# Sixteen of a modulation's 48 dot products moved ahead of the first attention

## The chip, the core and the metric

The kernel runs on one core of a Trainium2 chip. The core has five engines with instruction streams of their own: TensorE (PE: matmuls), VectorE (DVE), ScalarE (ACT), GpSimd (POOL) and SyncE (SP), which here only issues transfers. Each stream is written down when the program is built; the engines meet at semaphores. The metric is device time in microseconds (us), lower is better.

## The reference, cut to what matters

The kernel computes a two-layer diffusion trunk over 1024 latent tokens and 256 context tokens of width 1024, all in float32. Each layer derives a shift, a scale and a gate from a conditioning vector, modulates its input with them, projects it to queries, keys, values and a gate path, runs a windowed attention, and closes with a projection and a LayerNorm.

```
silu_c = silu(c);  silu_cc = silu(c_ctx)
for i in range(2):
    shift, scale, gate       = split(silu_c  @ w_ada[i] + b_ada[i], 3)    # latent tokens
    shift_c, scale_c, gate_c = split(silu_cc @ w_ada[i] + b_ada[i], 3)    # context tokens
    u  = h  * (1 + scale)   + shift
    uc = hc * (1 + scale_c) + shift_c
    y, yc = mixer_a(u, uc, ...) if i == 0 else mixer_b(u, uc, ...)
    h  = layer_norm(alpha * h  + gate   * y,  ...)
    hc = layer_norm(alpha * hc + gate_c * yc, ...)    # first layer only
```

What the change moves is a part of `silu_c @ w_ada` and `silu_cc @ w_ada`: the first layer's gate and the second layer's shift and scale, 3 x 1024 numbers for each of the two vectors. None of them is needed before the first layer's attention is nearly over.

## The kernel before, in words

**Numbers as pairs.** Every matmul operand is split into a high and a low part, and a product is three matmuls (high x high, high x low, low x high). So most evacuations of a PSUM tile are a copy on ACT (the high part) and a subtraction on DVE (the low part).

**The start.** The first layer's shift and scale are made on PE while the input comes in by eight blocks of 128 rows (`hraw`, 128x1280, four buffers, tag "hraw"). `u_make` modulates each block and splits it; `k_mm` and `v_mm` accumulate the keys and the first four token blocks of the values. When the eighth block is through, the keys stand in four PSUM tiles (`kps`, names `kp0_0`, `kp0_1`, `kp1_0`, `kp1_1`, latent tokens) and in a part of `kc` (context tokens), and the first values in `vps`.

**Evacuation of the keys and the values.** `rope_evac` takes a key tile through a shuffle on DVE (L500, into `rb`), a product with the cosines on DVE (L501, into `ra`), a product with the sines on POOL (L502, `rb`), and a sum on DVE (L503). `k_store` splits the sum: ACT writes the high part (L511) and DVE the low part (L512) of a tile `st`, of which there are two, and SP issues its store to the buffer `kdA` in memory. `v_evac` does the same for values (ACT L270, DVE L271, store to `vdA`). Meanwhile PE runs `vproj_pieces`, the remaining values by three PSUM tiles `pv-1_2`, `pv-1_3`, `pv-1_4` of 48 matmuls each.

**The queries.** Then comes `qprojA(0)`, the first two heads' queries: PSUM tiles `pj8_0`, `pj8_1` (24 matmuls of 512 columns each) and `pj8_2` (24 of 256 columns), and behind it the gate path `pj10_0`, `pj10_1`, `pj10_2`. These tiles and the ones of keys and values come from one pool of four PSUM tiles of 512 columns (tag "one"), so each waits until a tile before it has been read out.

**The first attention** runs by eight pairs of heads p, twenty steps each: scores on PE (`S_A`), bias, mask and minimum on DVE (L322), exponential on ACT (L329), normalisation on POOL (L334), transposes on PE (`T_A`) and their split (ACT L345, DVE L347), then the values' product (`pvA`). It needs the keys back from memory (`k_load`, into `kA`) and the values (`v_loadA`). Between the steps PE is filled with the projections of this pair's gate and the next pair's queries. `merge` interleaves the two lists.

**The dot products.** The modulation's 3072 numbers per vector are rows of `wadaT` (24 blocks j of 128 rows). One `dot_half(h, j)` takes half h of the columns of block j: a load of 128x512 (256 KB) into `gw`, a multiplication with accumulation on DVE for the latent vector (L681), a multiplication in place on POOL for the context vector (L682), and its sum on ACT (L663). The 48 are laid between the attention's steps by `SEG`, the number for each pair of heads. At each half's first one the silu of both vectors is made in `gh`.

**What sets the order.** The program's text gives the order; the tile framework then places each engine's instructions by priorities and by its own estimates, except those in `keep_in_program_order`. It also chooses which buffer of a tag a tile gets. An engine never takes an instruction ahead of one that stands before it in its stream, and neither does SP.

Of the kernel before, what the change touches and what calls it, by code (L numbers as in the profile page):

```python
# [11 lines left out]
F32 = mybir.dt.float32  # L12
F32R = mybir.dt.float32r
BF16 = mybir.dt.bfloat16
AF = mybir.ActivationFunctionType
ALU = mybir.AluOpType
# [3 lines left out]
P = 128  # L20
D = 1024
S = 1024
C = 256
T = S + C
# [13 lines left out]

GATED_LAST = 1 << 20

SEG = (7, 7, 7, 7, 7, 7, 6, 0)


def f32(ap):
# [38 lines left out]
def build(tc, i, out):  # L83
    nc = tc.nc
    mm = nc.tensor.matmul
    dma = nc.sync.dma_start
# [25 lines left out]
    dcol = cp.tile([P, 32, 2], F32, name="dcol")  # L112
# [4 lines left out]
    vdA = dr.tile([T, 4, P], F32, name="vdA")  # L117
# [107 lines left out]
    def vproj_pieces(j0, u, evac, b0=0):  # L225

        pieces = []
        state = {}  # L230

        def piece(b, t, kq):
            def run():
                j1 = j0 + 4 if j0 >= 0 else 8
                if b == b0 and t == 0 and kq == 0:
                    w.split(j1)
                    w.load(j1 + 2)
                if b == 4 and t == 1 and kq >= 2:
                    w.split(j1 + kq - 1)
                if t == 0 and kq == 0:  # L240
                    state[b] = psone(f"pv{j0}_{b}")
                pt = state[b][:, t * 256 : (t + 1) * 256]
                tok = slice((2 * b + t) * P, (2 * b + t + 1) * P)
                for kt in (2 * kq, 2 * kq + 1):
                    hi, lo = w.got[j0 + kt // 2 if j0 >= 0 else VALUES[kt // 2]]
                    sl = slice((kt % 2) * 256, (kt % 2 + 1) * 256)
                    lh, ll = u.at(kt, tok)
                    mm(pt, lh, hi[:, sl], start=kt == 0 and t == 0, stop=False)
                    mm(pt, lh, lo[:, sl], start=False, stop=False)
                    mm(pt, ll, hi[:, sl], start=False, stop=kt == KT - 1 and t == 1)  # L250
                if t == 1 and kq == 3:
                    evac(state.pop(b), b)

            return (6 * 109, run)

        for bs in ((0, 1), (2,), (3,), (4,)) if b0 == 0 and j0 == pos["Bv", 0] else [(b,) for b in range(b0, 5)]:
            for kq in range(4):
                pieces += [piece(b, t, kq) for b in bs for t in range(2)]
        return pieces
# [4 lines left out]
    def v_evac(pl, vd):  # L264
        def evac(pt, b):
            st = st_tile(pl)
            for t in range(2):
                v = st[:, t].rearrange("p (h l d) -> p h l d", h=4, l=2)
                src = pt[:, t * 256 : (t + 1) * 256].rearrange("p (h d) -> p h d", h=4)
                nc.scalar.activation(v[:, :, 0, :], src, AF.Copy, scale=0.5)  # L270
                nc.vector.scalar_tensor_tensor(v[:, :, 1, :], src, 0.5, f32(v[:, :, 0, :]), ALU.mult, ALU.subtract)  # L271
            t0 = 2 * b * P
            dma(vd[t0 : t0 + 2 * P].rearrange("(t p) h e -> p t (h e)", p=P), f32(st))

        return evac
# [13 lines left out]
    def merge(att, fill, lead=0.0):  # L289

        ta = sum(a[0] for a in att) or 1.0
        tf = sum(f[0] for f in fill)
        ia = jf = 0
        ca = cf = 0.0
        while ia < len(att) or jf < len(fill):
            need = att[ia][2] if ia < len(att) and len(att[ia]) > 2 else 0
            if jf < len(fill) and (ia == len(att) or jf < need or cf - lead <= ca * (tf - lead) / ta):
                cf += fill[jf][0]
                fill[jf][1]()
                jf += 1  # L300
            else:
                ca += att[ia][0]
                att[ia][1]()
                ia += 1
# [161 lines left out]
    uA = Tokens(up, "uA")  # L466
    ap_, ap_st = pool("apool", "right")
    pp, pp_st = pool("p0", "right")
# [150 lines left out]
    for kt in range(-1, KT + 1):  # L619
        if kt + 1 < KT:  # L620
            for n in range(3) if kt < 0 else (kt + 3,) if kt + 3 < KT else ():
                mod_load(n, upto[n])
                if n == 0:
                    w.split(2)
            if kt == 0:

                u_make(0)
                k_mm(0, slice(0, 2))
            mod_rows(kt + 1)
            if kt == 0:  # L630
                k_mm(0, slice(2, 6), True)
        if kt > 1:
            k_mm(kt - 1)
        if kt + 1 < KT:
            mod(kt + 1)
        if kt == 0:
            k_mm(0, slice(6, None), True)
        if kt < 0:

            warm(vps[:, 0:512], 12)  # L640
        if kt > 0:
            v_mm(kt - 1)
        if kt < KT and kt >= 0:
            if kt:
                u_make(kt)
            w.split(upto[min(kt + 1, 7)])
    dma(ident, i["ident"])
    dma(lnc, i["lnc"])
    dma(cos, i["cos"])
# [7 lines left out]
    gh, sums = [], []  # L657
# [7 lines left out]
    def dot_half(h, j):  # L665
        def run():
            dot_sum()
            if j == 0:
                gh.clear()
                for v in range(2):  # L670
                    t = px.tile([P, 512], F32, tag=f"gh{v}", bufs=1, name="gh")
                    dma(t, bass.AP(i["cr"].tensor, v * D + h * 512, [[0, P], [1, 512]]))
                    th = px.tile([P, 512], F32, tag="gw", bufs=2, name="gth")
                    nc.scalar.activation(th, t, AF.Tanh, scale=0.5)
                    nc.vector.scalar_tensor_tensor(t, th, 1.0, t, ALU.add, ALU.mult)
                    gh.append(t)
            acc = dhalf if h else dcol
            t = px.tile([P, 512], F32, tag="gw", bufs=2, name="gw")
            dma(t, i["wadaT"][j, :, h * 512 : (h + 1) * 512])
            o = ap_.tile([P, 512], F32, tag="ra", bufs=1, name="gj")  # L680
            nc.vector.tensor_tensor_reduce(o, t, gh[0], 0.5, 0.0, ALU.mult, ALU.add, accum_out=acc[:, j, 0:1])  # L681
            nc.gpsimd.tensor_tensor(t, t, gh[1], ALU.mult)  # L682
            sums.append((t, acc[:, j, 1:2]))

        return (0.0, run, 0)
# [9 lines left out]
            nc.vector.scalar_tensor_tensor(colB[:, v, :], scale, 1.0, lnc[:, 1, :], ALU.add, ALU.mult)  # L695
            nc.vector.tensor_tensor(colB[:, v, :], colB[:, v, :], shift, ALU.add)

    dots = [dot_half(h, j) for h in range(2) for j in range(24)]
    evs = []
    for c, (t0, n) in enumerate(CHUNKS):  # L700
        for nt in range(2):
            pt = kps[c, nt] if c < 2 else kc[:, nt * C : nt * C + C]
            evs.append((1.0, lambda nt=nt, pt=pt, t0=t0, n=n: rope_evac(k_store(nt), pp, 2)(pt, t0, n)))
    merge(evs, [])
    for b in range(2):
        v_evac(pp, vdA)(vps[:, b * 512 : (b + 1) * 512], b)
    merge([], vproj_pieces(-1, uA, v_evac(pp, vdA), 2))
    pp_st.close()
    pq, pq_st = pool("attA", "right")

# [164 lines left out]
    for p in range(8):  # L875
# [6 lines left out]
        if p < 7:  # L882
            n = len(att)
# [77 lines left out]
    for b in range(10):  # L961
# [5 lines left out]
        else:  # L967
            o = og_split(up, raw, "h2") if b % 2 else og_split(oa, raw, "og")
# [8 lines left out]
        g = gts[:, b // 8]  # L977
# [287 lines left out]
    for n, row in enumerate(rowsB):  # L1265
        ex = []
        if n < len(subsB):
            h, jp, r = subsB[n]
# [209 lines left out]
```

## Time and profile before

| | |
|---|---|
| runs | 1424.73, 1422.10, 1424.25 us; median 1424.25 us |
| span of the profiled execution | 1422.0 us; the median of the runs is 2.25 us above it |
| PE, DVE, ACT, POOL busy over the span | 98%, 69%, 51%, 44% |
| keys' evacuation and values' projection | from 57 us to 78 us of the span |
| queries' projection up to the first scores | 78 us to 95 us |
| first attention | 95 us to some 580 us |
| the 48 dot products | first load at 106.0 us, last sum at 517.5 us |

Only the span of the profiled execution is given, not a time of its own for it; the three runs and the span lie within 2.7 us. A row of the profile's timeline has the start, the duration, the engine, the line of the program, the operation and its tiles (written <- read, buffer numbers left out). A duration begins when the engine takes the instruction up, so it holds whatever the instruction waits for after that.

### The profile page before, as it was taken

What the parts mean: (1) busy time and instruction counts of PE and PEld (TensorE: products, weight loads), DVE (VectorE), ACT (ScalarE), POOL (GpSimd) and SP (SyncE); (2) the same over time, 40 slices, a digit from 0 to 9 for tenths busy, and PEclk for the clock granted to TensorE, in tenths of its full rate; (3) what the DMA queues carried; (4) which work ended last, traced back from release to release, by engine and by line L of the source; (5) the groups of instructions that cost most, each with busy time, mean ns of one, the idle gap of its engine ahead of it and who ended that gap; (6) DMA issues with size and microseconds to landing.
All of it is one profiled execution on the core that took longest, in us unless ns stands there. A gap on an engine that the chain in (4) does not pass through costs nothing. (4 is left out here: it accounts for less than half of the span.)

```text
span 1422.0 us, 25163 instructions
## 1 busy us (share of the span) xinstructions
PE 1386.9 (98%) x8816; PEld 1215.3 (85%) x8816; DVE 981.9 (69%) x2220; ACT 731.0 (51%) x1560; POOL 627.5 (44%) x776
## 2 busy tenths in 40 slices
PE   9999999999999999999999999999999999999996
PEld 6988898888988888888898899888988899887885
DVE  4658887878888788666433765565565565669598
ACT  4347776677776778432222555455455454558200
POOL 0326676667667667233311333333233232325583
PEclk9999999999999999999999999999999999999998
DMA  9472114123222124344287575465555564475763
GB/s 380 180 222 86 61 50 131 47 79 101 72 71 64 57 69 144 123 134 134 75 253 221 160 212 166 131 193 146 175 151 169 149 185 150 126 217 177 181 153 103
DMA packets 128141, 202.39 MB, mean 142 GB/s; under 512 B 9744, under 2 KB 66448, under 8 KB 128016
## 3 DMA queue, kind: packets, MB, share of 16 engines
q1 hardware_dynamic: 127872, 200.78, 46.8%
q8 instruction: 70, 1.15, 0.3%
q14 instruction: 55, 0.45, 0.1%
q10 hardware_dynamic: 144, 0.01, 0.0%
HBM read 145.18 MB, written 55.57 MB: 141 GB/s over the span
## 5 line engine op out<-in xcount | busy, mean ns | idle before, releaser
L334 POOL TENSOR_SCALAR s_B<-s_B,rs_B 128x640 f32<-128x640 f32 (+1 forms) x128 | 103.6, 810 | 288.3 <-DVE rs_B L333 267.8
L212 PE MATMUL pj<-uBh,wh 128*128 128x512 f32 (+1 forms) x448 | 175.9, 393 | 0.0
L213 PE MATMUL pj<-uBl,wh 128*128 128x512 f32 (+1 forms) x448 | 170.3, 380 | 0.0
L214 PE MATMUL pj<-uBh,wl 128*128 128x512 f32 (+1 forms) x448 | 170.1, 380 | 0.0
L329 ACT ACTIVATE s_B<-s_B,m_B 128x640 f32<-128x640 f32 (+1 forms) x128 | 102.9, 804 | 125.2 <-DVE m_B L322 125.0
L329 ACT ACTIVATE s_A<-s_A,m_A 128x641 f32<-128x641 f32 (+2 forms) x160 | 119.5, 747 | 83.2 <-DVE m_A L322 60.6
L168 POOL TENSOR_TENSOR wl<-wr,wh 128x512 fp32r<-128x512 f32 x65 | 88.5, 1363 | 158.6 <-ACT wh L163 146.9
L334 POOL TENSOR_SCALAR s_A<-s_A,rs_A 128x640 f32<-128x640 f32 (+2 forms) x160 | 128.8, 805 | 65.6 <-DVE rs_A L333 59.7
L322 DVE CUSTOM_DVE_ANT_0 s_A<-S_A,msk,nsk 128x640 f32<-128x640 f32 (+2 forms) x160 | 123.6, 774 | 32.1 <-PE S_A L769 17.9
L347 DVE TENSOR_TENSOR pt_B<-T_B,pt_B 128x640 fp32r<-128x640 f32 (+1 forms) x128 | 101.0, 789 | 60.5 <-ACT pt_B L345 60.1
L212 PE MATMUL pj<-uAh,wh 128*128 128x512 f32 (+1 forms) x384 | 140.1, 365 | 0.8 <-DVE otmp L808 0.8
L213 PE MATMUL pj<-uAl,wh 128*128 128x512 f32 (+1 forms) x384 | 137.7, 359 | 0.0
L214 PE MATMUL pj<-uAh,wl 128*128 128x512 f32 (+1 forms) x384 | 137.3, 357 | 0.0
L347 DVE TENSOR_TENSOR ptl_A<-T_A,pth_A 128x640 fp32r<-128x640 f32 (+2 forms) x160 | 114.1, 713 | 14.7 <-PE pvA L797 8.1
L341 PE MATMUL T_A<-ident,s_A 128*128 128x128 f32 x672 | 100.9, 275 | 10.7 <-DVE m_A L322 5.1
L345 ACT CAST pt_B<-T_B 128x640 fp32r<-128x640 f32 (+1 forms) x128 | 84.4, 659 | 48.5 <-PE T_B L341 47.4
L341 PEld LDWEIGHTS T_A<-ident,s_A 128*128 128x128 f32 x672 | 77.3, 140 | 37.1 <-issue 10.0
L322 DVE CUSTOM_DVE_ANT_0 s_B<-S_B,bias 128x640 f32<-128x640 f32 (+1 forms) x128 | 100.4, 784 | 8.2 <-PE S_B L1107 7.4
L345 ACT CAST pth_A<-T_A 128x640 fp32r<-128x640 f32 (+2 forms) x160 | 96.3, 602 | 15.8 <-PE T_A L341 14.4
L214 PEld LDWEIGHTS pj<-uBh,wl 128*128 128x128 f32 x448 | 84.3, 188 | 16.6
L213 PEld LDWEIGHTS pj<-uBl,wh 128*128 128x128 f32 x448 | 84.7, 189 | 9.1
L212 PEld LDWEIGHTS pj<-uBh,wh 128*128 128x128 f32 x448 | 84.5, 189 | 9.0
(224 smaller groups left out, 3874.2 us busy)
## 6 DMA issues: line engine op xcount, KB each, us to landing
kB<-kdB SPq DMA_DIRECT2D x64, 320.0 KB, 5.3
gw<-in_wadaT SPq DMA_DIRECT2D x48, 256.0 KB, 2.8
vdB<-st SPq DMA_DIRECT2D x20, 512.0 KB, 3.5
vB<-vdB SPq DMA_DIRECT2D x16, 640.0 KB, 4.5
wada<-in_wadaC SPq DMA_DIRECT2D x16, 512.0 KB, 9.6
kdB<-st SPq DMA_DIRECT2D x16, 512.0 KB, 2.8
qdB<-st SPq DMA_DIRECT2D x16, 512.0 KB, 3.6
qB<-qdB SPq DMA_DIRECT2D x32, 256.0 KB, 4.7
```

The source lines that it names most:

```text
L168: e.tensor_tensor(lo, r, f32(hi), ALU.subtract)
L212: mm(pt[:, :n], hi[:, sl], rh, start=kt == 0, stop=False)
L213: mm(pt[:, :n], hi[:, sl], rl, start=False, stop=False)
L214: mm(pt[:, :n], lo[:, sl], rh, start=False, stop=kt == KT - 1)
L322: nc.vector.tensor_tensor_reduce(outp, sc, in1, scale, init if init is not None else 3e38, ALU.add, ALU.min, accum_out=s.m)
L329: nc.scalar.activation(s.t[:, :n], s.t[:, :n], AF.Exp, bias=s.m, scale=-1.0, accum_out=s.sum)
L334: nc.gpsimd.tensor_scalar(s.t[:, : s.w], s.t[:, : s.w], s.rs, 1.0, ALU.mult, ALU.mult)
L341: nc.tensor.transpose(tp[:, k * P : (k + 1) * P], s.t[:, src * P : (src + 1) * P], ident)
L345: nc.scalar.copy(pt.hi[:, :n, hl, :], tv)
L347: nc.vector.tensor_tensor(pt.lo[:, :n, hl, :], tv, f32(pt.hi[:, :n, hl, :]), ALU.subtract)
```

## The change

`dot_early(j)` makes the first half of blocks 0 to 15 before the attention. Eight of these sixteen are written ahead of the keys' evacuation and eight among the pieces of the values' projection. They use the four buffers of the input, tag "hraw": one for the silu of both vectors (`gh`), one for what nobody reads (`gj`), and two in turn for the rows (`gw`, two blocks j by one load of 512 KB). The remaining 32 stay in the attention, five for each of the first four pairs of heads and four for each of the next three.

```diff
-SEG = (7, 7, 7, 7, 7, 7, 6, 0)
+SEG = (5, 5, 5, 5, 4, 4, 4, 0)
...
+    early, pending = [], []
+
+    def dot_early(j):
+        if not early:
+            t = pp.tile([P, T], F32, tag="hraw", bufs=4, name="gh")
+            g = t[:, 0:1024].rearrange("p (v d) -> p v d", v=2)
+            dma(g, bass.AP(i["cr"].tensor, 0, [[0, P], [D, 2], [1, 512]]))
+            o = pp.tile([P, T], F32, tag="hraw", bufs=4, name="gj")
+            th = o[:, 0:1024].rearrange("p (v d) -> p v d", v=2)
+            nc.scalar.activation(th, g, AF.Tanh, scale=0.5)
+            nc.vector.scalar_tensor_tensor(g, th, 1.0, g, ALU.add, ALU.mult)
+            early.extend((g, o))
+        g, o = early[:2]
+        if j % 2 == 0:
+            t = pp.tile([P, T], F32, tag="hraw", bufs=4, name="gw")
+            t = t[:, 0:1024].rearrange("p (j d) -> p j d", j=2)
+            dma(t, i["wadaT"][j : j + 2, :, 0:512].rearrange("j p d -> p j d"))
+            early[2:] = [t]
+        t = early[2][:, j % 2]
+        nc.vector.tensor_tensor_reduce(o[:, 0:512], t, g[:, 0], 0.5, 0.0, ALU.mult, ALU.add, accum_out=dcol[:, j, 0:1])
+        nc.gpsimd.tensor_tensor(t, t, g[:, 1], ALU.mult)
+        early_sum()
+        pending.append((t, dcol[:, j, 1:2]))
+
+    def early_sum():
+        if pending:
+            t, acc = pending.pop()
+            nc.scalar.activation(t, t, AF.Copy, scale=0.5, accum_out=acc)
+
+    for j in range(8):
+        dot_early(j)
     dma(ident, i["ident"])
...
-            if j == 0:
+            if not gh or gh[-1] != h:
...
+                gh.append(h)
...
-    dots = [dot_half(h, j) for h in range(2) for j in range(24)]
+    dots = [dot_half(0, j) for j in range(16, 24)] + [dot_half(1, j) for j in range(24)]
...
-    merge([], vproj_pieces(-1, uA, v_evac(pp, vdA), 2))
+    for n, (_, piece) in enumerate(vproj_pieces(-1, uA, v_evac(pp, vdA), 2)):
+        piece()
+        if n < 12 and n % 3 < 2:
+            dot_early(8 + n // 3 * 2 + n % 3)
+    early_sum()
```

In the changed program the early dot's reduction on DVE is L666, its product on POOL L667 and its sum on ACT L674.

**POOL, from the first key tile on.** Before, POOL has the four sine products (`rb`) and the low parts of four weight tiles (`wl8` to `wl11`) until the queries' first sine product:

```order
L168 TENSOR_TENSOR wl8_940<-wr8_794,wh8_939 128x512
L502 TENSOR_TENSOR rb_735<-rb_735,sin_138 128x512
L168 TENSOR_TENSOR wl9_956<-wr9_796,wh9_955 128x512
L502 TENSOR_TENSOR rb_745<-rb_745,sin_138 128x512
L502 TENSOR_TENSOR rb_755<-rb_755,sin_138 128x512
L168 TENSOR_TENSOR wl10_986<-wr10_983,wh10_985 128x512
L168 TENSOR_TENSOR wl11_992<-wr11_989,wh11_991 128x512
L502 TENSOR_TENSOR rb_765<-rb_765,sin_138 128x512
L502 TENSOR_TENSOR rb_1025<-rb_1025,sin_138 128x512
```

Eight instructions stand ahead of the queries' product `rb_1025`, and the trace of before runs these in this order. Now, from the same place:

```order
L502 TENSOR_TENSOR rb_771<-rb_771,sin_138 128x512
L667 TENSOR_TENSOR gw_731<-gw_731,gh_726 128x512 x2
L502 TENSOR_TENSOR rb_781<-rb_781,sin_138 128x512
L667 TENSOR_TENSOR gw_738<-gw_738,gh_726 128x512
L168 TENSOR_TENSOR wl8_1008<-wr8_830,wh8_1007 128x512
L667 TENSOR_TENSOR gw_738<-gw_738,gh_726 128x512
L168 TENSOR_TENSOR wl9_1024<-wr9_832,wh9_1023 128x512
L502 TENSOR_TENSOR rb_791<-rb_791,sin_138 128x512
L667 TENSOR_TENSOR gw_746<-gw_746,gh_726 128x512 x2
L502 TENSOR_TENSOR rb_801<-rb_801,sin_138 128x512
```

The same eight and the sixteen products of the early dots stand in one row; the other eleven products and `wl10`, `wl11` follow these rows, and only then the queries' first sine product.

**DVE, where the queries' first tile is taken over.** The tile `pj8_0` is read by its shuffle and its cosine product. Before, these stand among the evacuations of the values:

```order
L271 SCALAR_TENSOR_TENSOR st_788<-vps_147,st_788 128x4x64 x2
L271 SCALAR_TENSOR_TENSOR st_847<-pv-1_2_798,st_847 128x4x64 x2
L271 SCALAR_TENSOR_TENSOR st_902<-pv-1_3_853,st_902 128x4x64 x2
L500 STREAM_SHUFFLE rb_1025<-pj8_0_999 128x512
L271 SCALAR_TENSOR_TENSOR st_965<-pv-1_4_908,st_965 128x4x64
L501 TENSOR_TENSOR ra_1024<-pj8_0_999,cos_137 128x512
L271 SCALAR_TENSOR_TENSOR st_965<-pv-1_4_908,st_965 128x4x64
L503 TENSOR_TENSOR ra_1024<-ra_1024,rb_1025 128x512
L500 STREAM_SHUFFLE rb_1062<-pj8_1_1036 128x512
```

Now they stand behind the sixteenth reduction, whose two rows are the first here:

```order
L666 ISA gj_728,dcol_70<-gw_926,gh_726 128x512
L666 ISA dcol_70 128x1
L500 STREAM_SHUFFLE rb_1094<-pj8_0_1068 128x512
L501 TENSOR_TENSOR ra_1093<-pj8_0_1068,cos_137 128x512
L271 SCALAR_TENSOR_TENSOR st_904<-pv-1_2_834,st_904 128x4x64
L503 TENSOR_TENSOR ra_1093<-ra_1093,rb_1094 128x512
L271 SCALAR_TENSOR_TENSOR st_904<-pv-1_2_834,st_904 128x4x64
L271 SCALAR_TENSOR_TENSOR st_970<-pv-1_3_913,st_970 128x4x64 x2
L271 SCALAR_TENSOR_TENSOR st_1033<-pv-1_4_976,st_1033 128x4x64
L500 STREAM_SHUFFLE rb_1131<-pj8_1_1105 128x512
```

All sixteen reductions, the keys' evacuation and that of `vps` stand ahead of `pj8_0`, and the evacuations of the three `pv` tiles have moved behind it. With this the PSUM tiles have changed: `pj8_1` had the tile of `pv-1_2` before and has that of `pj8_0` now. On PE nothing changes up to the first scores but where these stand: behind 14 matmuls of `pj10_0` before, behind all 24 of `pj10_0` and 10 of `pj10_1` now.

**SP, where the first keys are loaded back.** Before, the loads of keys and values (`kA0`, `vA0`) follow the values' stores at once:

```order
L273 DMA vdA_74<-st_847 128x2x512
L273 DMA vdA_74<-st_902 128x2x512
L273 DMA vdA_74<-st_965 128x2x512
L742 DMA kA0_0_975<-kdA_73 64x1280 x2
L742 DMA kA0_1_978<-kdA_73 64x1280 x2
L747 DMA vA0_981<-vdA_74 128x10x128
L149 DMA wr14_1111<-in_wAg 128x512
L149 DMA wr15_1113<-in_wAg 128x512
```

Now two weight loads stand between:

```order
L273 DMA vdA_74<-st_904 128x2x512
L273 DMA vdA_74<-st_970 128x2x512
L273 DMA vdA_74<-st_1033 128x2x512
L149 DMA wr14_1180<-in_wAg 128x512
L149 DMA wr15_1182<-in_wAg 128x512
L779 DMA kA0_0_1044<-kdA_73 64x1280 x2
L779 DMA kA0_1_1047<-kdA_73 64x1280 x2
L784 DMA vA0_1050<-vdA_74 128x10x128
```

`wr14` and `wr15` have moved ahead of the keys; they take the buffers of `wr12` and `wr13`, which POOL reads last, behind the queries' second sine product. Further up in SP's row the eight loads of `gw` stand between the stores of `kdA`.

## The prediction

> **What bounds the kernel now.** First the page's busy times, then the table by stretches, then the rows at the places where the change puts its work.
>
> ```profile
> PE 1386.9 (98%) x8816; PEld 1215.3 (85%) x8816; DVE 981.9 (69%) x2220; ACT 731.0 (51%) x1560; POOL 627.5 (44%) x776
> 60.00:80.00 20.00, 20.00 (x163) 19.75 (x162) 13.94 (x20) 5.54 (x11) 8.47 (x6) 1.00 0.50 174
> 80.00:100.00 20.00, 20.00 (x104) 17.18 (x104) 12.23 (x23) 7.04 (x15) 7.26 (x7) 1.00 0.84 247
> 100.00:160.00 60.00, 55.67 (x363) 48.45 (x363) 51.70 (x125) 43.06 (x98) 41.54 (x57) 1.00 0.29 89
> 160.00:220.00 60.00, 58.64 (x385) 51.88 (x385) 48.64 (x119) 41.06 (x94) 40.47 (x59) 1.00 0.25 76
> ...
> 460.00:520.00 60.00, 58.42 (x384) 51.60 (x384) 49.41 (x129) 41.38 (x96) 34.41 (x55) 1.00 0.16 56
> 520.00:580.00 60.00, 58.72 (x382) 51.20 (x381) 47.69 (x109) 46.86 (x100) 38.00 (x54) 1.00 0.36 115
> ```
>
> A row has the stretch, its length, then PE, PEld, DVE, ACT and POOL busy. PE bounds: it is never idle from 60 to 100 us, where the sixteen dots go, and idle 4.33 us of the attention's first 60 (100 to 160). The six stretches from 160 to 520 with dots (first and last shown) leave 9.32 us idle, 1.55 each; the one without dots (520 to 580) leaves 1.28. So what a dot holds up in the attention is small, and where it goes nothing is free on PE: the question is whether DVE, POOL and SP can do it there without making PE wait.
>
> **What a dot costs.**
>
> ```profile
> L681 DVE CUSTOM_DVE_ANT_0 gj<-gw,gh x48: 671/692/1822, 111.5 to 514.7; 128x512 f32<-128x512 f32 x48
> L682 POOL TENSOR_TENSOR gw<-gw,gh x48: 1273/1290/1301, 112.3 to 515.7; 128x512 f32<-128x512 f32 x48
> L663 ACT ACTIVATE gw<-gw x48: 613/632/649, 113.6 to 517.0; 128x512 f32<-128x512 f32 x48
> L663 ACT ACTIVATION_READ_ACCUMULATOR gw<-gw x48: 181/187/207, 114.2 to 517.5; 128x1 f32 x48
> gw<-in_wadaT SPq DMA_DIRECT2D x48, 256.0 KB, 2.8
> vdB<-st SPq DMA_DIRECT2D x20, 512.0 KB, 3.5
> ```
>
> By the medians (ns): 0.69 us of DVE, 1.29 of POOL, 0.82 of ACT, and 2.8 us for a load; the doubled load is put at 3.3, an estimate between 2.8 for 256 KB and 3.5 for 512 KB. In the attention 16 dots fewer are worth at most a third of the idle time from 100 to 520, 13.65 x 16/48 = 4.6 us. Against the stretch without dots the excess is 6 x 0.27 us, a third of it 0.5, and this is nearer, since the waits stay when the dots are gone: I take 0.6 us gained.
>
> **How DVE and POOL share.** Rows from the keys' evacuation in time order, DVE first, then POOL; the last of each is a reduction and a product of dots.
>
> ```profile
> 57.20 0.73 DVE L500 STREAM_SHUFFLE rb<-kp 128x512 f32<-128x512 f32 x1
> 57.82 0.68 DVE L501 TENSOR_TENSOR ra<-kp,cos 128x512 f32<-128x512 f32 x1
> 59.33 1.75 DVE L503 TENSOR_TENSOR ra<-ra,rb 128x512 f32<-128x512 f32 x1 [0.16 <-POOL rb L502]
> 65.81 1.78 DVE L512 TENSOR_TENSOR st<-ra,st 128x512 fp32r<-128x512 f32 x1
> 67.51 1.77 DVE L503 TENSOR_TENSOR ra<-ra,rb 128x512 f32<-128x512 f32 x1
> 145.65 1.82 DVE L681 CUSTOM_DVE_ANT_0 gj<-gw,gh 128x512 f32<-128x512 f32 x1
> ```
>
> ```profile
> 58.01 1.29 POOL L502 TENSOR_TENSOR rb<-rb,sin 128x512 f32<-128x512 f32 x1 [2.58 <-DVE rb L500]
> 59.26 1.28 POOL L168 TENSOR_TENSOR wl<-wr,wh 128x512 fp32r<-128x512 f32 x1
> 60.49 1.75 POOL L502 TENSOR_TENSOR rb<-rb,sin 128x512 f32<-128x512 f32 x1
> 67.00 1.74 POOL L502 TENSOR_TENSOR rb<-rb,sin 128x512 f32<-128x512 f32 x1
> 145.64 1.29 POOL L682 TENSOR_TENSOR gw<-gw,gh 128x512 f32<-128x512 f32 x1
> ```
>
> A DVE operation with both inputs in SBUF does not run beside a POOL operation. The sum at 59.33 ends at 61.08, 0.6 us after POOL's 59.26 + 1.28; POOL's product at 60.49 ends 1.28 after that. At 145.65 the reduction takes 1.82 us because POOL took its product at 145.64. Operations that read PSUM (L500, L501) are not held up. Under contention the two alternate, 1.28 + 0.6 us a pair. In the attention this is rare (median 692 ns); ahead of it the early dots bring 16 of each in a row.
>
> **The walk through the start, term by term.** These are the rows where PE takes new PSUM tiles, and what must be done before.
>
> ```profile
> 66.94 0.28 PE L248 MATMUL pv-1_3_853<-wv,uAh 128*128 128x256 f32 x1
> 78.46 0.39 PE L212 MATMUL pj<-uAh,wh 128*128 128x512 f32 x1
> 83.91 0.39 PE L212 MATMUL pj<-uAh,wh 128*128 128x512 f32 x1
> 89.35 0.28 PE L212 MATMUL pj<-uAh,wh 128*128 128x256 f32 x1
> 92.23 0.40 PE L212 MATMUL pj<-uAh,wh 128*128 128x512 f32 x1
> 95.43 0.28 PE L768 MATMUL S_A<-kA,qA 128*128 128x256 f32 x1
> 83.11 0.42 DVE L271 SCALAR_TENSOR_TENSOR st<-pv-1_2_798,st 128x256 fp32r<-128x256 f32 x1 [0.45 <-ACT st L270]
> 85.52 0.73 DVE L500 STREAM_SHUFFLE rb<-pj 128x512 f32<-128x512 f32 x1
> ```
>
> `pj8_0` runs from 78.46 to 83.91 (24 matmuls, 0.227 us each), `pj8_1` to 89.35, `pj8_2` to 92.23, the scores start at 95.43. `pj8_1` needed the evacuation of `pv-1_2`, over at 83.53: 0.4 us to spare.
>
> 1. `pv-1_3` needs `kp0_1`, whose cosine product now stands behind four reductions. From 58.0 the alternation has passed six POOL operations and six of DVE's by 69.3 (6 x 1.88 = 11.3); the cosine product runs beside the sixth POOL operation, until 68.7. PE was ready at 66.94: it waits 1.8 us, so `pj8_0` runs from 80.2 to 85.7.
> 2. `pj8_1` now needs `pj8_0` itself read out, behind all reductions. Until the sixteenth is done, POOL has 22 operations to do (4 sine products, 4 weight parts, 14 dots) and DVE 24 with two SBUF inputs (16 reductions, 4 sums, 4 low parts): 22 x 1.28 + 24 x 0.6 = 42.6 us. I add 2.2 us for two places where the row stops for a tile `st` on its way to memory. Shuffle and cosine product take 1.3. So 58.0 + 42.6 + 2.2 + 1.3 = 104.1: `pj8_1` starts at 104.1 instead of 83.91, 20.2 us late, of which 18.4 is a wait behind `pj8_0`.
> 3. The first scores need `kA0`, now behind `wr14` and `wr15`. DVE first evacuates the three `pv` tiles: POOL's last two dots and the sine product, 3 x 1.28 from 102.8, hold the sum ahead of the second half of `pv-1_2`, which is done at 107.7; its `st` comes back from memory after 3.5, and 0.8 later half of `pv-1_4` is through, at 112.0. PE ends `pj8_1` at 104.1 + 5.45 plus up to 2.6 for a cold clock (below), 112.1 at most. Then shuffle 0.65, sine product 1.28, two weight parts with a turn of DVE's between 3.0 (117.0), and two issues of 0.59:
>
> ```profile
> L742 SPq DMA_DIRECT2D kA<-kdA x16: 444/587/1802, 89.0 to 454.1; - x16
> DMA to landing us min/median/max: 4.1/5.2/8.0
> 1.20 5.30 PE L480 MATMUL warm<-zero 128*128 128x512 bf16 x12 [1.20 <-DVE zero L476]
> 1410.00:1422.00 12.00, 0.05 (x1) 0.00 (x0) 7.77 (x16) 0.00 (x0) 0.92 (x1) 0.62 0.31 87
> ```
>
> So the first pair of `kA0` is issued by 118.2 and lands 5.2 us later: scores at 123.4. PE is there at 112.1 + 2.88 + 34 x 0.227 = 122.7, so clock and keys cost it about the same. Against 95.43, and less the 20 gate matmuls that it has done more by then (4.54 us), this is 123.4 - 99.97 = 23.4 us late. The cold clock: after its last matmul at 1410 the granted clock's mean over 12 us is 0.62, and the program's first twelve matmuls of 512 columns take 0.44 us each instead of 0.227; twelve such cost 2.6 us. Were PE warm, the keys would still come at 123.3.
> 4. The attention's first pair of heads has 20 matmuls less to fill PE with, where DVE is already busy 51.70 of 60 us. Lost between 0 and 4.5 us; I take 1.0, since DVE is also rid of two dots there.
> 5. Extra work, and what is moved past it on SP:
>
> ```profile
> 37.44 0.33 SPq L649 DMA_DIRECT2D cos<-in_cos  x1
> 57.20 0.01 DVE L500 LOAD_MASK_SELECT rb<-kp  x1 [1.74 <-PE kp L603]
> 61.12 0.62 ACT L511 CAST st<-ra 128x512 fp32r<-128x512 f32 x1 [6.63 <-DVE ra L503]
> ```
>
> The silu in `gh` (128x1024, some 1.2 us each of ACT and DVE, twice the dot's 512 columns) falls into the 6.63 us that ACT waits and the 1.74 that DVE waits ahead of 57.2: nothing, or 2 us without that gap. `cos` is issued one transfer later than at 37.44 and first used at 57.82. `wr8` and `wr9` now stand behind a `gw` that waits until the last input block is modulated, before 57.2, and are used at 80: covered.
>
> Sum: 23.4 - 0.6 + 1.0 = +23.8 us. The span goes from 1422.0 to 1445.8; the median of the runs, 2.25 us above the span, from 1424.25 to about 1448. A measurement of this kernel can tell about 0.2% (2.8 us) from no change.
>
> **A rule weighed against these rows.** By the medians of the dots' rows, 692 and 1290 ns, one would let the two engines run side by side, since half of those 48 reductions or more show no wait; the sum would be that of the first rival below, 1434. The Trainium skill, page "SBUF — State Buffer", section "SBUF: two separate sides", says that VectorE and GpSimd arbitrate for one pair of ports as "an exclusive lock, not a bandwidth split", that VectorE takes part with two SBUF inputs, and that the loser blocks for the whole instruction; by it all 22 and 24 operations follow one another and the sum is 1448. The trace agrees where both contend: 1.75, 1.78, 1.77 and 1.82 us, each POOL's end plus 0.6.
>
> **The rivals.**
>
> *Little contention (0.14).* If DVE's reductions slip between POOL's operations, POOL alone sets the pace: 20 x 1.28 from 58.0 to 83.6, a sum of 0.8, a last load of 3.3, two reductions 1.4, shuffle and product 1.3: 90.4 instead of 104.1, 13.7 us less, 1434. For it speaks that a dot's product waits for its own reduction, which takes turns out of the row; against it the three waits in a row from 65.81 on.
>
> *The loads set the pace (0.13).* Only two `gw` buffers turn: a load waits for both sums of the tile two before, and SP's row holds stores of `kdA` between. If a load takes the keys' 6.2 us or so instead of 3.3 (the longest landing among the keys' loads is 8.0), three of the six later turns get 3 us longer: 9 us more, 1457.
>
> *Faster (0.04).* The dots fit into the gaps and the attention gains: DVE is busy 13.94 of 20 us from 60 to 80, POOL 8.47. It is decided at `pj8_0`'s shuffle: if the sixteenth reduction is over by 84.4 instead of 102.8, PE does not wait there, and the attention's 4.6 us at most give 1419.7. Against it: sixteen products alone are 20.6 us of POOL, and from 58.0 with its eight others 30.7.
>
> *Nothing (0.03).* The first stretch's idle time (4.33 us) and the dots' share take back what the start loses, which then would have to be under 5 us, with the tile of `pj8_0` read out by 88.
>
> **How the numbers follow.** The forecast has 0.66, for 1440 to 1454. The range takes in the first two rivals, 1434 to 1457. Slower by over 0.2%: 0.66 + 0.14 + 0.13 = 0.93; within 0.2% 0.03; faster 0.04.
>
> **What would show it.** Right: PE waits some 2 us ahead of `pv-1_3` and 15 to 20 us ahead of `pj8_1`, for DVE's L501; L666 and L667 alternate, many L666 at 1.8 us; the first scores come near 123 us; attention from there on is shorter by 0 to 2 us once the gate matmuls are counted. Wrong: `pj8_1` starting before 95 us (no contention), or long gaps on DVE and POOL with SP waiting for ACT's L674 (loads), or an idle time of the attention that falls by over 4 us.

## The result, and the profile after

| | before | after |
|---|---|---|
| time, median of the runs (us) | 1424.24 | 1447.4 |
| ratio, 95% interval | | 1.0169, 1.0156 to 1.0182 |
| span of the profiled execution (us) | 1422.0 | 1446.2 |
| first / last scores (us) | 95.4 / 568.7 | 122.2 / 594.7 |

The kernel is slower by 22 to 26 us; 1448.0 was forecast, in a range of 1434 to 1457. The total came out, but not each of its terms. One execution of the run warm24 below took 5414.83 us at a granted clock of 0.25, and its time is the median of the other three.

First, what PE waits for up to 130 us (in all, times, longest), and then the rows where these waits end.

```profile
PE pj L212 <- DVE ra L501: 16.7, 1, 16.7
PE S_A L805 <- DMA kA<-kdA: 2.0, 1, 2.0
PE pv-1_3_913 L248 <- DVE ra L501: 1.0, 1, 1.0
```

```profile
68.22 0.39 PE L248 MATMUL pv-1_3_913<-wv,uAh 128*128 128x256 f32 x1 [1.04 <-DVE ra L501]
102.14 0.80 PE L212 MATMUL pj<-uAh,wh 128*128 128x512 f32 x1 [16.68 <-DVE ra L501]
122.18 0.36 PE L805 MATMUL S_A<-kA,qA 128*128 128x256 f32 x1 [2.00 <-DMA kA<-kdA]
```

The three waits that were forecast are there, in their places: one ahead of `pv-1_3`, the long one ahead of `pj8_1` (102.14 instead of 83.91), one for the keys.

DVE and POOL between 65 and 73 us, and the groups of the early dots (min/median/max in ns, first and last start):

```profile
65.78 1.77 DVE L666 CUSTOM_DVE_ANT_0 gj<-gw,gh 128x512 f32<-128x512 f32 x1
72.11 1.76 DVE L512 TENSOR_TENSOR st<-ra,st 128x512 fp32r<-128x512 f32 x1
65.27 1.74 POOL L667 TENSOR_TENSOR gw<-gw,gh 128x512 f32<-128x512 f32 x1
71.59 1.74 POOL L502 TENSOR_TENSOR rb<-rb,sin 128x512 f32<-128x512 f32 x1
...
L666 DVE CUSTOM_DVE_ANT_0 gj<-gw,gh x16: 681/1218/1774, 58.5 to 100.2; 128x512 f32<-128x512 f32 x16
L667 POOL TENSOR_TENSOR gw<-gw,gh x16: 1259/1644/1766, 60.1 to 101.9; 128x512 f32<-128x512 f32 x16
```

They do alternate here: 1.77 us on DVE, 1.74 on POOL, since each carries the other's turn. Over the whole row it is less: the median reduction took 1.22, not 1.8. An undisturbed operation of this size with two SBUF inputs takes 0.68 us on DVE; what these operations took above that, up to `pj8_0`'s shuffle at 100.79, adds up to 14.6 us (4.4 in the kernel before, up to its shuffle at 85.52). What DVE waited for from 58 to 101 us:

```profile
DVE st L271 <- ACT st L270: 3.1, 3, 1.8
DVE st L512 <- ACT st L511: 2.9, 2, 2.2
DVE gj L666 <- DMA gw<-in_wadaT: 0.3, 1, 0.3
```

In the kernel before, the first two of these waits were 5.2 and 4.2 us up to its shuffle at 85.52: DVE waits less for ACT now than it did, though fewer evacuations stand ahead of that shuffle.

Last, the stretches by engine (length, then PE, PEld, DVE, ACT and POOL busy, granted clock, DMA share, GB/s). The first and the last answer to the rows of before; the middle pair is the attention's beginning.

```profile
80.00:100.00 20.00, 5.46 (x25) 4.17 (x23) 13.68 (x22) 8.61 (x24) 14.27 (x10) 0.72 0.72 240
120.00:130.00 10.00, 7.02 (x27) 5.36 (x26) 2.66 (x7) 1.32 (x4) 0.00 (x0) 0.83 1.08 259
130.00:140.00 10.00, 7.31 (x35) 7.07 (x36) 6.20 (x17) 6.33 (x14) 4.63 (x8) 0.66 0.44 123
480.00:540.00 60.00, 58.73 (x384) 51.49 (x384) 48.13 (x120) 39.63 (x91) 35.75 (x56) 1.00 0.18 54
```

PE was busy 5.46 of the 20 us from 80 to 100, where it had no gap before. And what nobody forecast: from 120 to 140 us PE is idle 5.7 us, of which only 2.0 are the wait for the keys ahead of the scores, and its clock is granted at 0.83 and 0.66.

### The profile page after: what moved, and what is told of

It is laid out like the page before. It is cut to its first block, busy times and chain, and to the rows that moved or that the text cites. A ratio compares the mean times of both kernels' runs of the same rounds, so it can differ in the third digit from the quotient of the medians.

```text
span 1446.2 us, 25144 instructions
## 1 busy us (share of the span) xinstructions
PE 1392.0 (96%) x8815; PEld 1220.6 (84%) x8816; DVE 987.6 (68%) x2221; ACT 733.2 (51%) x1561; POOL 628.2 (43%) x776
## 5 line engine op out<-in xcount | busy, mean ns | idle before, releaser
L329 ACT ACTIVATE s_B<-s_B,m_B 128x640 f32<-128x640 f32 (+1 forms) x128 | 102.9, 804 | 126.2 <-DVE m_B L322 125.9
L212 PE MATMUL pj<-uAh,wh 128*128 128x512 f32 (+1 forms) x384 | 141.7, 369 | 16.7 <-DVE ra L501 16.7
L345 ACT CAST pth_A<-T_A 128x640 fp32r<-128x640 f32 (+2 forms) x160 | 96.5, 603 | 20.7 <-PE T_A L341 19.1
L248 PE MATMUL pv<-wh,uBh 128*128 128x256 f32 x320 | 92.1, 288 | 0.0
```

The source lines that it names most:

```text
L212: mm(pt[:, :n], hi[:, sl], rh, start=kt == 0, stop=False)
L329: nc.scalar.activation(s.t[:, :n], s.t[:, :n], AF.Exp, bias=s.m, scale=-1.0, accum_out=s.sum)
L345: nc.scalar.copy(pt.hi[:, :n, hl, :], tv)
```

## The experiments

All but wada4p, which was made from the kernel before, were made from the changed kernel; each was run against the kernel before. To compare them, each profiled span is cut into three. *Start* is how much later the first scores begin than at 95.4, less 0.227 us for each matmul that PE has done more by then (n of the projection `pj10` stand ahead of the scores; 14 before). *Attention* is the time from the first to the last scores against before's 473.3, plus the same 0.227 us for each matmul already done. *Rest* is what lies behind. The three add up to the change of the span.

| kernel | n | first scores | start | attention | rest | ratio, 95% interval |
|---|---|---|---|---|---|---|
| changed kernel | 34 | 122.2 | +22.3 | +3.7 | -1.8 | 1.0169, 1.0156 to 1.0182 |
| no_early: no early dots at all | 14 | 95.0 | -0.4 | -3.1 | +0.7 | 0.9968, 0.9957 to 0.998 |
| no_pool: early reductions on DVE only | 34 | 111.6 | +11.7 | -0.3 | -1.4 | 1.0084, 1.0067 to 1.01 |
| no_dve: early products on POOL and sums only | 28 | 114.3 | +15.7 | -2.3 | -1.7 | 1.0082, 1.0066 to 1.0098 |
| dve_only: both products of a dot on DVE | 28 | 117.5 | +18.9 | -0.8 | -1.1 | 1.0113, 1.0098 to 1.0127 |
| eight: the first eight early dots | 28 | 116.2 | +17.6 | +1.4 | -1.5 | 1.0121, 1.0106 to 1.0137 |
| eight_v: eight, behind the keys | 18 | 106.1 | +9.8 | -0.1 | -0.2 | 1.0077, 1.0061 to 1.0094 |
| wada4p: four, on POOL | 16 | 105.4 | +9.5 | -0.6 | -2.6 | 1.0054, 1.0041 to 1.0067 |
| no_sum: without ACT's sums | 28 | 119.3 | +20.7 | -2.6 | -0.3 | 1.012, 1.0106 to 1.0135 |
| warm24: 24 matmuls more ahead of `pj8_1` | 17 | 116.7 | +20.6 | -4.6 | +2.1 | 1.0126, 1.0109 to 1.0143 |
| pre16: 16 matmuls more in `pj8_0` | 23 | 119.9 | +22.5 | -3.3 | -0.4 | 1.0138, 1.0122 to 1.0154 |
| warm64: 64 matmuls more ahead of `pj8_1` | 3 | 118.8 | +25.9 | -2.4 | +0.1 | 1.0168, 1.0153 to 1.0183 |

Each row's three terms come from one execution; the *rest* scatters from -2.6 to +2.1 with no cause that I looked for, so differences of 2 us in a term are not to be read.

### What the attention gains by a third fewer dots

```diff
-    for j in range(8):
-        dot_early(j)
...
-            dot_early(8 + n // 3 * 2 + n % 3)
+            pass
```

> Leaves out the sixteen early dots altogether (their loads, reductions, products and sums); the attention keeps its 32. PSUM tiles and SP's row fall as in the kernel before. It bounds what a third fewer dots can be worth to the attention. My theory (all of the loss is in the stretch ahead of the first scores, the attention gains 0.6): first scores near 95.5 us, time 1423.6 us, ratio 0.9985 to 1.0005. Rival (dots are what holds the attention up): 1419.7 us, ratio 0.9968. Second rival (the new order of the attention itself costs something): over 1428 us with the first scores unmoved.

1419.19 us, 2.8 to 6.1 us faster than before: the rival's figure. PE's stretch from 120 to 180 us, first of the kernel before, then of this one:

```profile
120.00:180.00 60.00, 56.35 (x363) 49.44 (x364) 51.51 (x125) 43.58 (x101) 42.97 (x60) 1.00 0.19 61
...
120.00:180.00 60.00, 58.43 (x383) 51.49 (x383) 49.26 (x122) 42.04 (x95) 41.96 (x59) 1.00 0.17 54
```

By the runs a dot costs the attention some 0.2 to 0.4 us, and this one stretch has 2.1 of the 3.1 us that the profile shows. My 0.6 us for all sixteen was wrong; the bound of 4.6 lies inside the measured interval, so it is neither shown nor refuted. So there was something to win, and it was not seen in the changed kernel.

### One half of the early dots at a time

```diff
-        nc.gpsimd.tensor_tensor(t, t, g[:, 1], ALU.mult)
-        early_sum()
-        pending.append((t, dcol[:, j, 1:2]))
```

> Of each early dot only the reduction on DVE is made; the product on POOL and its sum on ACT (half of the dot products) are left out. pj8_1 still takes pj8_0's PSUM tile and stands behind all sixteen reductions, kA0 stands behind wr14 and wr15, as in the changed kernel. My theory (DVE and POOL exclude each other, so the loss is the two engines' work laid end to end): with 14 products fewer to alternate with, 14 x 1.28 = 18 us go from the row, pj8_0 is read out at 84 to 88 us instead of 102, PE waits 0 to 3 us there, scores at 100 to 107 us, time 1424 to 1432 us. Rival (DVE's own amount of work and its order are what is late): pj8_0 read out after 95 us, time over 1438 us.

```diff
-        nc.vector.tensor_tensor_reduce(o[:, 0:512], t, g[:, 0], 0.5, 0.0, ALU.mult, ALU.add, accum_out=dcol[:, j, 0:1])
```

> Of each early dot only the product on POOL and its sum on ACT are made; the reduction on DVE (the other half of the dot products) is left out. pj8_1 takes pv-1_2's PSUM tile, as in the kernel before. My theory (mutual exclusion): POOL's 16 products stay, 20.5 us more on POOL; its row ends near 57 + 30 x 1.28 + some waits = 96 to 100 us, the sine product of pj8_0 and with it the keys come 8 to 13 us late: time 1431 to 1438 us. Together with the run without POOL's half the two losses then sum to less than the 23 us of the whole. Rival (POOL is the bound by itself): 1443 us or more. Rival (loads of gw set the pace): PE's start as late as in the changed kernel, 1445 us.

```diff
-        nc.gpsimd.tensor_tensor(t, t, g[:, 1], ALU.mult)
-        early_sum()
-        pending.append((t, dcol[:, j, 1:2]))
+        nc.vector.tensor_tensor_reduce(o[:, 512:1024], t, g[:, 1], 0.5, 0.0, ALU.mult, ALU.add, accum_out=dcol[:, j, 1:2])
```

> The same computation as the changed kernel, with the early dots' second product made as a second reduction on DVE too: 32 reductions on DVE, no early product on POOL, no sum on ACT. pj8_1 takes pj8_0's PSUM tile and stands behind all 32. My theory (it is the 1.28 us of each POOL product inside DVE's row that costs): a dot takes 2 x 0.69 = 1.4 us of DVE instead of 1.28 + 0.6 = 1.9, and needs no sum on ACT: pj8_0 read out near 93 to 97 us instead of 102, time 1438 to 1443 us, ratio to the kernel before 1.010 to 1.013. Rival (what costs is the amount of work in front of pj8_0 on DVE): 16 reductions more, no better than the changed kernel, 1447 us or more. Rival (loads of gw): 1447 us as well, with DVE waiting for loads.

1436.14, 1435.94 and 1440.31 us. (Lines of the first two stand one further down than in the changed kernel.) What PE waits for: one line of the run without POOL's half, one of the run without DVE's, two of the run with all on DVE.

```profile
PE pj L213 <- DVE ra L502: 8.0, 1, 8.0
...
PE pj L213 <- DVE st L272: 11.8, 1, 11.8
...
PE pv-1_3_900 L248 <- DVE ra L501: 9.9, 1, 9.9
PE pj L212 <- DVE ra L501: 3.4, 1, 3.4
```

DVE's row in the run without POOL's half shows the exclusion as one would want it: 0.68 us where POOL is idle, 1.78 where POOL has its own sine product at 67.04.

```profile
66.78 0.68 DVE L667 CUSTOM_DVE_ANT_0 gj<-gw,gh 128x512 f32<-128x512 f32 x1
67.39 1.78 DVE L504 TENSOR_TENSOR ra<-ra,rb 128x512 f32<-128x512 f32 x1
69.09 0.68 DVE L667 CUSTOM_DVE_ANT_0 gj<-gw,gh 128x512 f32<-128x512 f32 x1
```

But the sum falls short of the theory. Without POOL's half `pj8_0` is read out at 91.8 us, not at 84 to 88, and the time is above the 1424 to 1432 us that I expected; with everything on DVE it is read out at 99.4, not at 93 to 97, though that time, 1440.31, lies where I expected it. Without DVE's half the time, 1435.94, does so too, but the first scores are 18.9 us later, where 8 to 13 were expected of the keys. And the two halves alone cost 11.9 and 11.7 us, together 23.6, as much as both in one kernel (23.2); in the start alone they cost 11.7 and 15.7, more than the 22.3 of both. A price that came only from early reductions meeting early products would show in the whole and not in its halves. So each half already stands in front of work that PE waits for, and by different ways. Without POOL's half, the reductions' own time, 16 x 0.68 = 11 us, is in DVE's row. Without DVE's half, DVE waits 17.4 us for ACT's casts up to `pj8_0`'s shuffle at 95.49, where it waited 9.4 before, and POOL waits 5.1 us for loads between its products. Making the second product on DVE does gain (16 us of loss instead of 23), but sixteen reductions now stand ahead of `kp0_1`'s cosine product and PE waits 9.9 us already at `pv-1_3`.

### Fewer dots, and other places

```diff
-SEG = (5, 5, 5, 5, 4, 4, 4, 0)
+SEG = (6, 6, 6, 6, 6, 5, 5, 0)
...
-            dot_early(8 + n // 3 * 2 + n % 3)
+            pass
```

> Only the first eight dots (those ahead of the keys' evacuation) are made early; the other 40 stay in the attention. Whole computation. pj8_1 takes pv-1_2's PSUM tile, kA0 stands between wr14 and wr15, the scores behind 24 + 4 matmuls. My theory (each pair of a product and a reduction takes 1.28 + 0.6 us of one common row): 8 pairs less than in the changed kernel, 15 us, so pj8_0 is read out near 87 us, pj8_1 waits 1 to 4 us, time 1428 to 1434 us. Rival (loss in proportion to the number of dots): half of 23, 1436 us. Rival (what costs is that dots stand ahead of the keys): pv-1_3 late by 5 us or more, 1438 us.

The same with the loop of the first eight taken out instead, and those eight made among the values' projection:

> Only eight dots early, all of them among the values' projection, none ahead of the keys' evacuation; the other 40 stay in the attention. Whole computation. pj8_1 takes pv-1_2's PSUM tile, kA0 stands ahead of wr14 and wr15, the scores behind 18 matmuls. My theory: the same 8 pairs, 15 us of the common row, partly in the time that DVE and POOL have free from 60 to 100 us: pj8_1 waits 0 to 3 us, time 1425 to 1431 us. Rival (the number of dots decides, not where they stand): the same time as with the first eight. Rival (the gain of the attention shows at last): below 1423 us.

And four dots, both products on POOL, in the buffers of the modulation's weights:

```diff
+    gh0 = pp.tile([P, 4, 2 * P], F32, tag="wada", bufs=10, name="gh").rearrange("p a b -> p (a b)")
...
+            nc.gpsimd.tensor_tensor(o[:, x], t[:, x], g[:, 0], ALU.mult)
+            nc.gpsimd.tensor_tensor(t[:, x], t[:, x], g[:, 1], ALU.mult)
+            nc.scalar.activation(o[:, x], o[:, x], AF.Copy, scale=0.5, accum_out=dcol[:, j + x, 0:1])
+            nc.scalar.activation(t[:, x], t[:, x], AF.Copy, scale=0.5, accum_out=dcol[:, j + x, 1:2])
```

> Another place: only four dots early, both products of each on POOL, the sums on ACT, no reduction on DVE; in buffers of the modulation's weights, which are free before the input's, so that POOL's products can start near 49 us, where POOL is idle. 44 dots stay in the attention. Whole computation. Theory (a dot is free only where DVE and POOL are both free): half of the eight products fall ahead of 57 us, four (5.1 us) stand between the keys' evacuation, pj8_1 0 to 3 us late, and the attention gains 1: 1422 to 1428 us, ratio 0.999 to 1.003. Rival (POOL idle is enough): 1421 to 1423 us.

1441.31, 1434.2 and 1432.2 us, all three outside what I had expected. Half the dots cost four fifths of the start (17.6 of 22.3 us) ahead of the keys, and 9.8 behind them; a quarter of the dots still cost 9.5. Rows of the run with the first eight, behind its last reduction (DVE, ACT and SP):

```profile
85.66 1.34 DVE L512 TENSOR_TENSOR st<-ra,st 128x512 fp32r<-128x512 f32 x1 [2.96 <-ACT st L511]
91.28 0.42 DVE L512 TENSOR_TENSOR st<-kc,st 128x256 fp32r<-128x256 f32 x1 [3.94 <-ACT st L511]
...
83.88 0.63 ACT L674 ACTIVATE gw<-gw 128x512 f32<-128x512 f32 x1 [2.67 <-POOL gw L667]
85.02 0.61 ACT L511 CAST st<-ra 128x512 fp32r<-128x512 f32 x1
90.88 0.37 ACT L511 CAST st<-kc 128x256 fp32r<-128x256 f32 x1 [4.07 <-DMA kdA<-st]
...
87.33 4.76 SPq L513 DMA_DIRECT2D kdA<-st  x3
```

Here nothing is short of an engine. DVE waits until 85.66 for ACT's cast into a tile `st`. That cast stands on ACT behind the sum of the last early product, which waited for POOL until 83.88, and behind a cast of weights. DVE's subtraction ends at 87.00, the tile's store is issued at 87.33, and ACT waits for that store until 90.88. With two `st` tiles, cast, subtraction and store follow one another, and what is late ahead of this chain is late behind it. The second half of `pv-1_2` is read out at 97.45 instead of 83.11, and `pj8_1` waits 12.8 us for it. Of these 14.3 us, 10.9 lie ahead of the keys' last sum (80.93 instead of 69.99), where the dots stand in DVE's row, and 3.4 in the chain behind it.

The run with four dots says the same. It never got the quiet place that it was made for: POOL's first product is at 55.5 us, since the silu in `gh` stood in ACT's and DVE's rows behind the last input block. So POOL's eight products stand among its sine products, and DVE waits for these:

```profile
DVE ra L503 <- POOL rb L502: 3.0, 3, 1.3
```

Before, this wait was 0.2 us. The keys' last sum starts at 74.10 instead of 69.99, and the second half of `pv-1_2` at 90.14 instead of 83.11: 4.1 us lost ahead of the chain, 2.9 in it. DVE's waits for ACT's casts from 58 to 101 us hardly differ (11.1 us, 10.3 before). Whether POOL being idle is enough, and whether a dot ahead of 55 us would be free, was not tried.

### Are ACT's sums what holds the row?

```diff
-        early_sum()
-        pending.append((t, dcol[:, j, 1:2]))
```

> Reductions and products of the sixteen early dots stay, their sums on ACT are left out (so half of these dot products is missing). By the trace of the changed kernel DVE waits 6.0 us for ACT's casts into st between 90 and 100 us, and ACT itself stands there in sums that wait for POOL. pj8_1 takes pv-1_2's PSUM tile, the scores stand behind 28 matmuls. Theory (part of the row is not the alternation of DVE and POOL but ACT's sums in front of its casts): pj8_1 starts at 94 to 98 us instead of 102, time 1436 to 1441 us. Rival (the alternation alone, as the prediction had it): pj8_1 at 100 us or later, 1444 to 1448 us.

1441.57 us. DVE's waits for ACT from 58 to 101 us fell from 6.0 to 2.5, but those for loads rose from 0.3 to 2.0, and the wait ahead of `pj8_1`, now for `pv-1_2`'s evacuation, ended at 101.7, hardly earlier than 102.1:

```profile
PE pj L213 <- DVE st L272: 12.5, 1, 12.5
```

The theory falls for the start, 20.7 us late. The 5.8 us that this kernel is faster lie in the attention (-2.6 against +3.7), which the sums don't explain; the next runs bear on that.

### The order of the keys, and PE's clock

```diff
+    def warm_gap():
+        t = psbig("warmgap")
+        x = uA.at(0, slice(0, 512))[0]
+        for _ in range(24):
+            tc.keep_in_program_order(mm(t[:, 0:512], x[:, 0:P], x, start=True, stop=True))
...
+    merge([], q0[:8] + [(0.0, warm_gap, 0)] + q0[8:])
```

> The changed kernel with 24 matmuls more whose result nobody uses, on PE between pj8_0 and pj8_1 (5.4 us in the 16.7 us that PE waits there). By the order kA0 then stands ahead of wr14 and wr15 on SP, and the scores behind 17 matmuls of pj10_0 instead of 34. The wait ahead of pj8_1 stays (it ends with DVE's L501 at 102 us), the clock still falls in its last 11 us. My theory in the prediction (kA0 behind wr14 and wr15 sets the scores): scores at 115 to 117 us instead of 122, and the 17 matmuls that stay behind fill the first pair of heads: 1441 to 1445 us. Rival (only when pj8_1 starts counts; the matmuls are the same in the end): 1446 to 1449 us.

The same with 64 for 24:

> As the run with 24 matmuls more, but 64 of them (14.5 us): PE is busy nearly to the end of the wait and its clock is full when pj8_1 starts; the scores stand behind 3 matmuls of pj10_0. Theory that the clock costs (after the trace of the changed kernel: granted clock 0.50 from 102 to 106, 122 to 126 and 132 to 140 us, about 7 us of half speed, so some 3.5 to 5 us lost): scores at 111 to 114 us, granted clock 1.00 from 102 to 180, time 1438 to 1442 us, less than with 24. Rival (as in the prediction, the clock costs nothing beside the keys): the same as with 24 within 1.5 us.

```diff
+                if j0 == pos["Aq", 0] and ci == 0 and kq == 0:
+                    hi, lo = w.got[j0]
+                    for _ in range(16):
+                        mm(pt[:, :n], hi[:, 0:P], u.at(0, slice(t0, t0 + n))[0], start=True, stop=True)
```

> The changed kernel with 16 matmuls more whose result nobody uses, at the start of pj8_0 (3.6 us, out of the 16.7 us that PE waits behind it). PE is cold when pj8_1 starts, as in the changed kernel; what differs is the order: kA0 stands ahead of wr14 and wr15 on SP, the scores behind 23 matmuls instead of 34, and 11 matmuls more are left to fill the first pair. It separates this order from the 24 matmuls that ran right ahead of pj8_1. Theory (the order of kA0 and the filling of the first pair are what 5.7 us hung on): pj8_1 at 102 us, scores at 116 to 118 us, granted clock 1.00 from 118 to 180, time 1441 to 1444 us. Rival (the clock at pj8_1's start did it): 1445 to 1448 us.

1441.49, 1447.54 and 1443.4 us. With 24, time and first scores (116.7) are those of the theory; with 16 the time is, but the scores are not (119.9, and `pj8_1` starts at 104.4); with 64 neither figure came. In the run with 64 the matmuls write a PSUM tile that is read out only at 93.5 us, so they ran until 109.8 and `pj8_1` came late behind them.

```profile
93.57 16.43 PE L916 MATMUL warmgap<-uAh 128*128 128x512 f32 x64 [8.17 <-DVE st L512]
```

The run with 16 tells most. PE waits 15.8 us for `pj8_1` and the first scores are 22.5 us late, as in the changed kernel (22.3); and yet it is faster by 4 us, all of it in the attention. Its rows for the stretches shown above of the changed kernel:

```profile
120.00:130.00 10.00, 9.18 (x51) 7.33 (x49) 5.36 (x15) 4.52 (x10) 2.36 (x4) 1.00 0.60 150
130.00:140.00 10.00, 9.30 (x70) 8.57 (x70) 8.60 (x19) 7.49 (x17) 5.48 (x9) 1.00 0.43 120
```

Granted clock 1.00 against 0.83 and 0.66 (1.7 + 3.4 = 5.1 us of full speed), PE idle 1.5 us against 5.7, 2.0 of which are the changed kernel's wait for the keys. What differs is the order: 11 matmuls more are left to put between the first scores and transposes, and the scores do not wait for the keys. PE then hardly falls idle, and its clock is not cut.

The other runs tell idle time and clock apart. All nine kernels here have 32 dots in the attention; idle time and granted clock are those of the 20 us from each one's first scores, and the lost clock is 20 us times what the clock falls short of 1.

| kernel | n | PE idle | granted clock | lost clock | idle + lost | attention |
|---|---|---|---|---|---|---|
| changed kernel | 34 | 3.8 | 0.74 | 5.2 | 9.0 | +3.7 |
| no_pool | 34 | 3.8 | 0.91 | 1.8 | 5.6 | -0.3 |
| dve_only | 28 | 2.5 | 0.91 | 1.8 | 4.3 | -0.8 |
| warm64 | 3 | 3.4 | 1.00 | 0 | 3.4 | -2.4 |
| no_dve | 28 | 2.6 | 1.00 | 0 | 2.6 | -2.3 |
| no_sum | 28 | 2.6 | 1.00 | 0 | 2.6 | -2.6 |
| pre16 | 23 | 1.5 | 1.00 | 0 | 1.5 | -3.3 |
| warm24 | 17 | 0.5 | 1.00 | 0 | 0.5 | -4.6 |
| no_early | 14 | 0.5 | 1.00 | 0 | 0.5 | -3.1 |

The attention's term is the sum of the two less 4.8 to 5.9 us in the first eight rows, and less 3.6 in the last, which has the most idle time behind its first 20 us (11.8 us, 9.4 to 11.2 in the others). So, as an account, the clock weighs more in the changed kernel, 5.2 us against 3.8. The run without POOL's half has the same n and the same idle time and still loses 4.0 us less, so n alone does not set it. In the changed kernel the clock is at 0.50 twice: from 122.8 to 126.2 us, behind the 2.0 us of waiting for the keys, and from 133.0 to 139.9, behind waits of 1.9 and 1.2 us ahead of the first transposes. No run changed the clock alone.

That kA0 goes ahead of `wr14` and `wr15` did not bring the scores forward by itself: in the run with 16 the PE was the later (119.9, no wait for keys), in the run with 24 the keys again (116.7, wait of 1.9).

## Why the prediction was right, point by point

1. `pv-1_3`: 1.8 us of wait forecast, 1.04 measured; `pj8_0` ended at 85.5 (forecast 85.7). Right.
2. `pj8_1`: 104.1 forecast, 102.14 measured, the wait 16.7 for 18.4. Right in size, not in its make-up. The Trainium skill, page "SBUF — State Buffer", section "SBUF: two separate sides", has the lock, and the trace agrees with it operation by operation (0.68 us alone, 1.77 against POOL). But the forecast let DVE wait out all of POOL's 22 operations, 28.2 us, and DVE was held up 14.6. What made up for it stood at nothing or less in the sum: DVE was idle 6.3 us instead of 2.2, and its operations that read PSUM (shuffles, cosine products, evacuations) took some 6.6 us of the row. That these errors cancel to 2 us is luck. Against the kernel before, DVE's row from the keys' first shuffle to that of `pj8_0` is 15.2 us longer (43.5 for 28.3): 19.1 for the reductions, 11 of them their own time, less 3.3 of idle time and less 1.6 of evacuations now behind it, and 1.0 more for the rest.
3. First scores: 123.4 forecast, 122.18 measured; late by 22.3 instead of 23.4. The last wait was for the keys (2.0 us), as forecast, with PE ready just those 2.0 us earlier. That the cold clock ahead of `pj8_1` costs nothing there holds within these 2 us.
4. The first pair of heads: 1.0 us forecast, at most 4.5. This is the step that failed. The attention came out 3.7 us longer where sixteen dots fewer gain 3.1: 6.8 us lost. I counted the 20 matmuls that were missing as filling, not that PE's clock falls when PE waits there: 5.2 us of clock, 1.7 of them behind the wait for the keys and the rest behind the waits among the first transposes.
5. The gain of the dots: 0.6 forecast, 3.1 by the profile and 2.8 to 6.1 by the runs without them. Too small: it was read from the stretches behind the attention's first, and most of it lies in that first one.
6. The costs at nothing (`gh`, `cos`, `wr8`, `wr9`): no wait shows for them up to `pv-1_3`, where PE waits less than forecast. Right as far as the trace shows.

So the sum of +23.8 met the span's +24.2 partly by luck: the attention, forecast at -0.6 + 1.0 = +0.4, came to -3.1 + 6.8 = +3.7, and that excess of 3.3 us was taken back by 1.1 us less in the start and by 1.8 us behind the attention, which had no term. The rival of little contention (1434) fell with `pj8_1` at 102.1, loads as the pace with 0.3 us of waiting for them, and the two by which nothing is lost at `pj8_0`'s shuffle, at 100.8 instead of 84 to 88 at most.

No version that does the whole work beats the kernel before. Even with four dots (1432.2 us) the start loses 9.5 us, and all sixteen could give back about 5.

## What to carry to other kernels

A busy share of 14 in 20 us is not room for 6 us of work when the engine's instructions are turns in a chain through other engines and stores, and when another engine can hold them up: ask what stands behind each place in the row, not how full the row is. When work that fills PE is moved ahead of a stage, look at that stage's first steps, where PE then waits between dependent steps and pays twice, in idle time and in clock (here 3.8 and 5.2 us). And leave the moved work out altogether in one run before building on its gain: it gave the ceiling (5 us) that no placement could pass.

## What was unexpected of the hardware

PE's clock fell after a short wait. One microsecond each, in the changed kernel (PE busy first, granted clock third from the end):

```profile
120.00:121.00 1.00, 0.18 (x1) 0.00 (x0) 0.91 (x2) 0.14 (x1) 0.00 (x0) 1.00 1.12 244
121.00:122.00 1.00, 0.00 (x0) 0.00 (x0) 0.00 (x0) 0.00 (x0) 0.00 (x0) 1.00 0.95 210
122.00:123.00 1.00, 0.82 (x5) 0.83 (x6) 0.00 (x0) 0.00 (x0) 0.00 (x0) 0.90 1.00 220
123.00:124.00 1.00, 1.00 (x4) 0.73 (x3) 0.00 (x0) 0.00 (x0) 0.00 (x0) 0.50 1.00 192
126.00:127.00 1.00, 1.00 (x5) 0.80 (x4) 0.00 (x0) 0.00 (x0) 0.00 (x0) 0.89 1.11 336
```

PE was busy throughout 112 to 120, idle for 2.0 us, and then ran at half speed from 122.8 to 126.2, after it had work again. The run without sums shows it too: 2.3 us of wait ahead of `pj8_0`, granted clock 0.85 and 0.50 in the two microseconds from 82 on. The Trainium skill, page "TensorE: Matmul & The Clock Gate", section 'Part 1: The HAM clock gate (the "warmup" mystery)', gives half speed after at least one idle window of about 3.4 us; here 2.0 us of idleness were enough, and the stretch at half speed, 3.4 us, is one such window. Not every short wait does it: in the run with 24, PE waits 1.9 us for the keys ahead of its first scores at 116.7, and the clock stays at 1.00; in the run with 16, PE is busy 0.71, 0.56, 0.81 and 0.62 of the four microseconds from 128 on, and the clock stays at 1.00 there too. Where the bound lies was not tried.
